# Whole-row background norms, a two-chunk join and recut last groups in a decoder trunk on one core

## The chip, the core and the metric

One core of a Trainium2 chip runs the whole program. The metric is the time of one execution in microseconds, the median of several runs. The profile is of one execution.

## The reference

A decoder trunk of one layer works on 2064 prompt rows (16 learned ones and 2048) and on 64 sample rows (8 sequences of 8), all of 1024 channels. The layer has two sub-layers with residual adds, and a final norm follows. Everything is in float32.

```python
h = rmsnorm(x, norm1_g)
z = h @ w_in                                   # 1024 -> 5120
a = za * sigmoid(zg); a = causal_dwconv(a, prev_conv, conv_dw)      # width 31
a = silu(layernorm(a + conv_b, ln_g, ln_b)) @ w_conv_out
p = multiscale_pool(zp); p = (p @ w_pool per group) * pool_scale
x = x + (sigmoid(gate_a) * a + sigmoid(gate_b) * p) @ w_out
h2 = rmsnorm(x, norm2_g)
up = causal_dwconv(h2 @ w_up, prev_ffn, ffn_dw)                     # 1024 -> 5632, width 3
x = x + (gelu(g) * v) @ w_down                                      # 2816 -> 1024
y = rmsnorm(x, final_g)                        # x * rsqrt(mean(x*x) + 1e-6) * g
```

Outputs are y for the prompt and the sample rows, and the last rows of the three histories.

## The kernel before, in words

Channels lie on the 128 partitions and rows along the free axis. The rows are cut into three blocks of 704, 704 and 708 columns (the sample rows are in the last); a block is worked through in two halves of 352 or 354 columns, which fit the two halves of one PSUM tile. Every matrix product is done as three products of high and low parts (`hi` and `lo` in the type float32r), so a weight tile holds both parts.

A *unit* is the work of one chunk of 128 output channels: 48 matmuls for a projection from 1024 channels. The list `units` is the order of TensorE's work: for each block the input projection, the convolution's output, `WO` (the output projection), `FF` (the feed-forward), with parts of the next block in between. `WO` and `FF` of the first and the last block start with half units (`SPLIT`: first half, then second half); the middle block takes both halves at once. After each unit's matmuls a *post* empties its PSUM tile (four of them) with VectorE and ScalarE operations.

`join(i)` marks all units after unit i as joined to it. Joined units are issued in turns, one step over 128 input channels of each in a turn, so that a group can begin while the norm that feeds it is still giving out its channels. Between the turns of a joined group, and after each single unit, `drip()` issues background work. In `FF` (line 1402) the first three chunks, `up(0)`, `up(FC)` and `up(1)`, are one joined group for each part.

Background work is written as generators (`Task`). They give up control with `at(ap, late)`, "not before this tile is ready, plus `late`", by the kernel's own timetable (`Pace`), and with `room(k)`, "not before k tiles of the pool `spool` are free". `CALM` is 2.5 us of `late` for norms that nobody waits for. The order of the tasks in `order` is their priority; at the end all that are left are forced in this order. Posts come first, then weight splits, then these tasks.

A norm's factor is made by `rstd_ps` (line 361): `sumsq` squares and adds the eight channel tiles; small full-precision matmuls with the sum's columns as weights give the sums for 128 rows at a time in a PSUM column; ten VectorE operations on these few columns compute the inverse root; and more small matmuls spread each value over all 128 partitions. `rstd_of` copies that to SBUF. A block of 704 or 708 columns takes six slices, a half three. Tasks with norms are `norm1_rstd` (first norm of a block), `norm2`, `final`, and `conv_norm` for the LayerNorm.

Weights come through four buffers (`W_BUFS`); SP issues their loads in order, three units ahead when the split parts are already kept in DRAM. In the last block (`MIXED`) all but the first three of the 22 feed-forward chunk pairs are made by a scheme with seven half-size products (`pair`), and the residual is kept in DRAM between the down-projections: `fetch` reads it, `spill` writes it back.

```python
MIX_GROUPS = (6, 6, 4, 3, 3)     # chunks for each down-projection of the last block
...
                    if f1 < FC - MIX_GROUPS[-1] and b in MIXED:
                        spill(b, c)
```

So in the last block a down-projection follows one pair after its chunks; the last but one and the last come after all pairs, the last one in halves (`SPLIT`). Helpers in the profile: L224 matmul, L183 tensor_tensor, L187 scalar_tensor_tensor, L192 and L194 tensor_scalar, L198 activation, L203 POOL copies, L207 loads by SP, L212 loads by POOL, L218 stores.

Of the kernel before, what the change touches and what calls it, by code (L numbers as in the profile page):

```python
# [8 lines left out]
F32 = mybir.dt.float32  # L9
F32R = mybir.dt.float32r  # L10
I32 = mybir.dt.int32
AF = mybir.ActivationFunctionType
ALU = mybir.AluOpType
# [5 lines left out]
FC = F // P  # L19
# [10 lines left out]
EPS = 1e-6  # L30
MAGIC = float(0x5F3759DF)

NBLK = 3
SBLK = 2
# [17 lines left out]
W_BUFS = 4  # L52
RAW_BUFS = 2
PLAIN = 3
MIX_GROUPS = (6, 6, 4, 3, 3)
MIX_ROOM = 4
F_GROUPS = (6, 5, 5, 6)
LEAD = 4
# [5 lines left out]
CALM = 2500.0  # L64
# [5 lines left out]
BOTH, FIRST, SECOND = (0, 1), (0,), (1,)  # L70
SPLIT = (FIRST, SECOND)
# [64 lines left out]
def trunk(ctx: ExitStack, tc: tile.TileContext, A, O):  # L136
# [15 lines left out]
    def S(cols, dt=F32, what="s"):  # L152
        assert cols <= S_COLS
        t = spool.tile([P, cols], dt, tag="s", name=nm(what))
        held.append(t)
        return t
# [3 lines left out]
    def room(k):  # L160


        def ok():
            held[:] = [t for t in held if sys.getrefcount(t) > 3]
            return len(held) + k <= S_SLOTS - RESERVE

        if not ok():
            yield "room", ok

    def PSUM():  # L170
        return pace.alloc("ps", 4, ppool.tile([P, 2, 512], F32, tag="ps", name=nm("ps")))
# [10 lines left out]
    def tt(out, a, b, op):  # L182
        nc.vector.tensor_tensor(out=out, in0=a, in1=b, op=op)  # L183
        pace.put("dve", dve(out, 68 + 60 * (b.space == "PSUM")), [out], [a, b])

    def stt(out, a, s, b, op0, op1):
        nc.vector.scalar_tensor_tensor(out=out, in0=a, scalar=s, in1=b, op0=op0, op1=op1)  # L187
        pace.put("dve", dve(out, 68 if isinstance(s, float) else 129), [out], [a, b])

    def ts(out, a, s1, s2, op0, op1=None):  # L190
        if op1 is None:
            nc.vector.tensor_scalar(out=out, in0=a, scalar1=s1, scalar2=None, op0=op0)  # L192
        else:
            nc.vector.tensor_scalar(out=out, in0=a, scalar1=s1, scalar2=s2, op0=op0, op1=op1)  # L194
        pace.put("dve", dve(out, 130, 1.92), [out], [a])

    def act(out, a, func, **kw):
        nc.scalar.activation(out, a, func, **kw)  # L198
        ptr = sum(not isinstance(v, float) for v in kw.values())
        pace.put("act", size(out) / 1.2 + 93 + 93 * ptr + 51 * (a.space == "PSUM"), [out], [a])  # L200
# [22 lines left out]
    def mm(out, lhsT, rhs, start, stop, rate=1.0, again=False):  # L223
        nc.tensor.matmul(out, lhsT=lhsT, rhs=rhs, start=start, stop=stop, skip_group_check=again)  # L224
        pace.put("pe", size(out) * rate / 2.4 + (15.5 if rate == 1.0 else 2.5), [out], [lhsT, rhs])

    cst = cpool.tile([P, NCST], F32, tag="cst", name="cst")
    half = cpool.tile([P, O_FD - O_LG], F32, tag="half", name="half")
    ones = cpool.tile([P, P], F32, tag="ones", name="ones")
    ahist = cpool.tile([P, KC, HC], F32, tag="ahist", name="ahist")  # L230
    phist = cpool.tile([P, KC, HP], F32, tag="phist", name="phist")
    hhist = [cpool.tile([P, KC, 2], F32R, tag=f"hhist{i}", name=f"hhist{i}") for i in range(2)]
# [36 lines left out]
    R = {}  # L269
# [108 lines left out]
    def at(ap, late=0.0):  # L378
        return "at", pace.ready(ap) + late
# [9 lines left out]
    def rstd_ps(src, n, late=0.0):  # L389
# [31 lines left out]
        yield at(ps)  # L421
        return ps[:, :halves, :h]

    def rstd_of(src, n, late=0.0):
        ps = yield from rstd_ps(src, n, late)
        yield from room(1)
        out = S(n)
        act(wide(out, ps), ps, AF.Copy)
        yield at(out)
        return out  # L430

    def wide(x, ps):
        return x.rearrange("p (a c) -> p a c", a=ps.shape[1])

    def sumsq(src, n):

        acc, prev = None, None
        for c in range(KC + 1):
            q = None
            if c < KC:  # L440
                s = yield from src(c)
                yield from room(1)
                q = S(n)
                act(q, s, AF.Square)
                del s
            if prev is not None:
                yield at(prev)
                if acc is None:
                    acc = prev
                else:  # L450
                    tt(acc, acc, prev, ALU.add)
            prev = q
        return acc
# [45 lines left out]
    def norm1_rstd(b):  # L499
        W = WIDTHS[b]  # L500
        yield from room(3)
        xs = [x_load(b, c) for c in range(2)]

        def src(c):
            x = xs.pop(0)
            if c + 2 < KC:
                xs.append(x_load(b, c + 2))
            yield at(x)
            return x

        R["rstd1", b] = yield from rstd_of(src, W, CALM)

    def h_make(b, last):
        while ("rstd1", b) not in R:
# [291 lines left out]
    def x_part(b, ts_, key):  # L806
        c0, c1 = cols(b, ts_)

        def src(k):
            c = order_of(ts_)[k]  # L810
            ok = lambda: all(c in R.get((key, b, t), ()) for t in ts_)
            while not ok():
                yield "cond", ok
            x = R["x1", b, c][:, c0:c1]
            yield at(x)
            return x

        return src
# [299 lines left out]
    def final(b, ts_):  # L1118
        c0, c1 = cols(b, ts_)
        last = b == NBLK - 1 and ts_[-1] == 1  # L1120
        r = yield from (rstd_ps if last else rstd_of)(x_part(b, ts_, "x2n"), c1 - c0, 0.0 if b == NBLK - 1 else CALM)
        for c in range(KC):
            x = R["x1", b, c][:, c0:c1]
            o = wide(x, r) if len(r.shape) == 3 else x
            calm = lambda: b == NBLK - 1 or pace.free["dma"] < pace.free["pe"]
            yield "room", calm
            stt(o, o, col(O_FG + c), r, ALU.mult, ALU.mult)
            store(O["y"][c, :, COL0[b] + c0 : COL0[b] + c1], x, b == NBLK - 1)
            if ts_[-1] == 1:
                del R["x1", b, c]  # L1130
            yield
# [25 lines left out]
    def join(first):  # L1157

        for u in units[first + 1 :]:
            u.joined = True  # L1160
# [197 lines left out]
    def FF(b, parts, last_parts):  # L1358

        mark["FF", b] = len(units)  # L1360
        ws = [w_up(0), w_up(FC), w_up(1)]
        holds = [[] if len(parts) > 1 else None for _ in ws]
        for ts_ in parts:
            i = len(units)
            for m, w, hold in zip((0, FC, 1), ws, holds):
                up(b, m, w, (("h2", b, ts_),), ts_, hold)
            join(i)
        nd = (("h2", b, parts[-1]),)
        f0, pend = 0, None
        for gs in MIX_GROUPS if b in MIXED else F_GROUPS:  # L1370
            for f in range(f0, f0 + gs):
                if b in MIXED and f >= PLAIN:
                    pair(b, f)
                else:
                    if f > 1:
                        up(b, f, w_up(f), nd + ((("mx", b),) if b in MIXED and f == PLAIN - 1 else ()))
                    if f:
                        up(b, FC + f, w_up(FC + f), nd)
                if f == (f0 if f0 + gs < FC or b not in MIXED else FC - 1) and pend:
                    DN(b, *pend)  # L1380
                    pend = None
            pend = (f0, f0 + gs)
            f0 += gs
        mark["up_end", b] = len(units)
        DN(b, *pend, last_parts)
# [18 lines left out]
    for b in range(NBLK):  # L1404
        if b + 1 < NBLK:
            add_task(("r1", b + 1), norm1_rstd(b + 1), mark["WO", b] if b else 2)
            add_task(("h1", b + 1), h_make(b + 1, False), mark["WO", b] if b else 0, [("r1", b + 1)])
        if b == 0:
            add_task(("cv", 0), conv_norm(0))
        add_task(("s", b), silu(b), mark["mid", b] if b else mark["C", 0] - 2, [("cv", b)])  # L1410
        for ts_ in parts.get(b, (BOTH,)):
            add_task(("h2", b, ts_), norm2(b, ts_))
        if b in MIXED:
            add_task(("mx", b), mixed_rows(b), after=[("h2", b, parts[b][-1]), ("mw",)])
        for ts_ in SPLIT if b == NBLK - 1 else (BOTH,):
            add_task(("y", b, ts_), final(b, ts_), mark["PG", b + 1] + 6 if b + 1 < NBLK else 0)
        if b + 1 < NBLK:
            add_task(("h1b", b + 1), h_make(b + 1, True), mark["up_end", b], [("r1", b + 1)])
        if b + 1 < NBLK:
            if b + 1 == SBLK:  # L1420
                for c in range(KC):
                    add_task(("sc", c), sample_conv(c))
            add_task(("cv", b + 1), conv_norm(b + 1), after=[("sc", c) for c in range(KC)] if b + 1 == SBLK else ())
# [76 lines left out]
    with tc.manual_schedule():  # L1500
# [10 lines left out]
        last = {}  # L1511
# [7 lines left out]
        i = 0  # L1519
        while i < len(units):  # L1520
# [25 lines left out]
            i = e  # L1546
# [95 lines left out]
```

## Time and profile before

| | |
|---|---|
| median of 3 runs | 2948.03 us (2946.34 to 2948.48) |
| profiled execution | 2945.39 us, span 2943.6 us, mean granted clock 0.996 |
| TensorE busy | 2902.4 us (99%), 17928 matmuls |
| VectorE busy | 2040.3 us (69%) |
| ScalarE busy | 817.5 us (28%) |
| GpSimd busy | 388.2 us (13%) |
| moved by DMA | 655.55 MB, mean 223 GB/s |

TensorE sets the time: in the chain that ended last its matmuls are 86%. To judge an edit, ask first whether it takes matmul time away, then which of TensorE's few waits it touches.

### The profile page before, as it was taken

To read this page: it belongs to the slowest core of one execution; us is meant where nothing else is said; L and a number is where in the kernel's file an instruction comes from. 1 tells how busy PE (TensorE), PEld (TensorE's weight loads), DVE (VectorE), ACT (ScalarE), POOL (GpSimd) and SP (SyncE) were. 2 spreads that over 40 slices of the span, in tenths; PEclk is the share of its full clock that TensorE was granted. 3 is DMA by queue.
4 is the path that set the end of the run, shared out by engine and by line. 5 is a ranking of instruction groups with operands and counts; after the bars stand their busy time and mean duration, and the time that the engine had idled before them with its cause. 6 is when DMAs were issued, how large, how long until landed. Compare 5 with 4: busy or idle time off the path is not lost.

```text
span 2943.6 us, 44436 instructions
## 1 busy us (share of the span) xinstructions
PE 2902.4 (99%) x17928; PEld 2895.6 (98%) x17928; DVE 2040.3 (69%) x3015; ACT 817.5 (28%) x1238; POOL 388.2 (13%) x752
## 2 busy tenths in 40 slices
PE   7999999999999999999999999999999999999998
PEld 7999999999999999999999999999999999999997
DVE  7999988679997454743498999656683136544556
ACT  4201334233223232522220212223252113221222
POOL 1111210120000001332110000223330010000000
PEclk9999999999999999999999999999999999999999
DMA  7424554865656655798644344779984365788786
GB/s 275 163 79 162 208 198 172 324 230 174 233 185 211 225 187 210 269 339 294 224 172 149 120 148 143 260 264 323 339 299 149 131 260 190 265 283 271 261 314 205
DMA packets 158397, 655.55 MB, mean 223 GB/s; under 512 B 25072, under 2 KB 37232, under 8 KB 116592
## 3 DMA queue, kind: packets, MB, share of 16 engines
q1 hardware_dynamic: 105728, 411.60, 41.7%
q0 software_dynamic: 52464, 241.11, 20.8%
q8 instruction: 141, 2.31, 0.3%
q14 instruction: 64, 0.52, 0.0%
HBM read 428.58 MB, written 224.05 MB: 222 GB/s over the span
## 4 chain that ended last, share of the span: by engine, by line
PE 86%; issue 4%; DVE 4%; DMA 3%; ACT 1%; POOL 1%; SPq 0%; DVEq 0%; POOLq 0%; ACTq 0%
PE ps L224 86%; DVE s L187 2%; POOL keep L218 1%; DMA raw<-in_w_out 1%; DVE s L183 1%; ACT s L198 1%; DVE wb L183 1%; DMA wb<-keep 1%; DMA keep<-s 1%; ACT wb L198 0%; DMA raw<-in_w_in 0%; SPq L207 0%; DMA cst<-in_cst 0%; DMA raw<-in_w_up 0%; POOL raw L212 0%
## 5 line engine op out<-in xcount | busy, mean ns | idle before, releaser
L224 PE MATMUL ps<-s,wb 128*128 128x354 f32 (+3 forms) x17628 | 2870.5, 325 | 12.6 <-DMA wb<-keep 4.1
L224 PEld LDWEIGHTS ps<-s,wb 128*128 128x128 f32 x17628 | 2858.3, 189 | 17.1 <-issue 8.7
L187 DVE SCALAR_TENSOR_TENSOR s<-s,half,s 128x704 f32<-128x704 f32 (+1 forms) x720 | 619.4, 923 | 0.3 <-ACT s L198 0.3
L198 ACT ACTIVATE s<-s 128x704 fp32r<-128x704 f32 (+10 forms) x447 | 313.5, 711 | 769.8 <-DVE s L187 484.1
L183 DVE TENSOR_TENSOR s<-s,s 128x704 fp32r<-128x704 f32 (+11 forms) x526 | 401.1, 775 | 123.4 <-ACT s L198 115.0
L183 DVE TENSOR_TENSOR s<-s,ps 128x704 f32<-128x704 f32 (+4 forms) x233 | 165.2, 720 | 251.8 <-PE ps L224 210.8
L198 ACT ACTIVATE s<-ps 128x356 f32<-128x356 f32 (+6 forms) x197 | 117.2, 601 | 658.2 <-PE ps L224 630.9
L187 DVE SCALAR_TENSOR_TENSOR s<-ps,cst,s 128x704 f32<-128x704 f32 (+1 forms) x188 | 178.1, 949 | 76.3 <-ACT s L198 72.4
L218 POOL DMA_DIRECT2D keep<-s x266 | 142.5, 541 | 587.8 <-ACT s L198 466.2
L187 DVE SCALAR_TENSOR_TENSOR s<-s,cst,s 128x708 f32<-128x708 f32 (+4 forms) x188 | 156.3, 842 | 69.2 <-ACT s L198 60.9
L183 DVE TENSOR_TENSOR wb<-raw,wb 128x1024 fp32r<-128x1024 f32 (+3 forms) x136 | 152.7, 1125 | 42.5 <-ACT wb L198 41.9
L198 ACT ACTIVATE wb<-raw 128x1024 fp32r<-128x1024 f32 (+3 forms) x136 | 132.3, 978 | 170.3 <-PE ps L224 66.4
L218 POOL DMA_DIRECT2D keep<-wb x136 | 77.1, 567 | 693.5 <-DVE wb L183 670.1
L198 ACT ACTIVATE s<-ps,cst 128x704 f32<-128x704 f32 (+1 forms) x94 | 78.9, 842 | 262.8 <-PE ps L224 257.4
L183 DVE TENSOR_TENSOR s<-raw,s 128x512 fp32r<-128x512 f32 x114 | 75.1, 686 | 95.6 <-ACT s L198 63.6
L187 DVE SCALAR_TENSOR_TENSOR s<-s,ps 128x704 f32<-128x704 f32 (+6 forms) x66 | 43.9, 685 | 132.8 <-PE ps L224 121.4
L187 DVE SCALAR_TENSOR_TENSOR s<-s,s 128x704 f32<-128x704 f32 (+2 forms) x96 | 84.8, 886 | 44.3 <-ACT s L198 42.6
L198 ACT ACTIVATE s<-raw 128x512 fp32r<-128x512 f32 x114 | 68.6, 625 | 124.9 <-DMA raw<-in_w_up 92.7
L183 DVE TENSOR_TENSOR s<-s 128x718 f32<-128x718 f32 (+6 forms) x64 | 55.0, 859 | 29.8 <-ACT s L198 22.5
L218 POOL DMA_DIRECT2D out_ffn_s<-sf x44 | 23.7, 538 | 301.6 <-ACT sf L198 250.2
L187 DVE SCALAR_TENSOR_TENSOR sc<-sa,cst,sc 128x64 f32<-128x64 f32 x232 | 46.9, 276 | 1.0 <-ACT sc L198 0.7
L198 ACT ACTIVATE s<-s,half 128x704 f32<-128x704 f32 (+1 forms) x48 | 46.4, 972 | 0.8
(62 smaller groups left out, 470.8 us busy)
## 6 DMA issues: line engine op xcount, KB each, us to landing
wb<-keep SPq DMA_DIRECT2D x225, 1024.0 KB, 4.9
keep<-wb POOLq DMA_DIRECT2D x100, 1024.0 KB, 6.5
keep<-s POOLq DMA_DIRECT2D x266, 256.0 KB, 5.1
wb<-keep SPq DMA_DIRECT2D x32, 768.0 KB, 4.8
raw<-in_w_up SPq DMA_DIRECT2D x44, 512.0 KB, 4.1
raw<-in_w_in SPq DMA_DIRECT2D x40, 512.0 KB, 4.6
raw<-in_w_up POOLq DMA_DIRECT2D x38, 512.0 KB, 9.2
wb<-keep SPq DMA_DIRECT2D x35, 512.0 KB, 4.7
```

Source lines behind the costliest of these rows:

```text
L183: nc.vector.tensor_tensor(out=out, in0=a, in1=b, op=op)
L187: nc.vector.scalar_tensor_tensor(out=out, in0=a, scalar=s, in1=b, op0=op0, op1=op1)
L198: nc.scalar.activation(out, a, func, **kw)
L218: (nc.sync if last else nc.gpsimd).dma_start(out=dst, in_=src)
L224: nc.tensor.matmul(out, lhsT=lhsT, rhs=rhs, start=start, stop=stop, skip_group_check=again)
```

## The change

It has five edits. `rstd_wide` makes a norm's factor on whole rows: `mean_of` splits the sum of squares into a high and a low part and multiplies each by a matrix of 1/1024, so that the mean stands on all partitions at once, with two products for each half; the inverse root is then computed on all columns by VectorE, with two squares on ScalarE. Three norms use it: the first norm of the last block, and the final norms of the first two blocks. The final norms of the last block keep the old helpers. `join(i)` is called after the second chunk of `FF`, so that `up(1)` follows as a unit of its own in each part. The down-projections of the last block take 6, 6, 3, 3 and 4 chunks. And the tasks for the two halves of the last block's final norm are listed second half first.

```diff
-MIX_GROUPS = (6, 6, 4, 3, 3)
+MIX_GROUPS = (6, 6, 3, 3, 4)
...
+    ones_r = ones.bitcast(F32R)
...
+    def mean_of(x, n):
+
+        yield from room(2)
+        hi, lo = S(n, F32R), S(n, F32R)
+        act(hi, x, AF.Copy)
+        yield at(hi)
+        tt(lo, x, hi.bitcast(F32), ALU.subtract)
+        yield at(lo, CALM)
+        ps = PSUM()
+        k = 1 if n <= 512 else 2
+        for t in range(k):
+            c = slice(t * (n // k), (t + 1) * (n // k))
+            mm(ps[:, t, : n // k], ones_r, lo[:, c], True, False)
+            mm(ps[:, t, : n // k], ones_r, hi[:, c], False, True)
+        return ps[:, :k, : n // k]
+
+    def rstd_wide(src, n):
+
+        acc = yield from sumsq(src, n)
+        yield at(acc)
+        ps = yield from mean_of(acc, n)
+        del acc
+        yield at(ps)
+        yield from room(4)
+        v, m, r = S(n), S(n), S(n)
+        ts(wide(v, ps), ps, EPS, None, ALU.add)
+        ts(r.bitcast(I32), v.bitcast(I32), -0.5, MAGIC, ALU.mult, ALU.add)
+        act(m, r, AF.Square)
+        yield at(m)
+        stt(m, m, -1.0, v, ALU.mult, ALU.mult)
+        q = S(n)
+        ts(q, m, 0.375, 1.25, ALU.mult, ALU.add)
+        yield
+        tt(q, q, m, ALU.mult)
+        stt(r, q, 1.875, r, ALU.add, ALU.mult)
+        act(m, r, AF.Square)
+        yield at(m)
+        stt(m, m, -0.5, v, ALU.mult, ALU.mult)
+        stt(r, m, 1.5, r, ALU.add, ALU.mult)
+        yield at(r)
+        return r
...
-        R["rstd1", b] = yield from rstd_of(src, W, CALM)
+        R["rstd1", b] = yield from (rstd_wide(src, W) if b == SBLK else rstd_of(src, W, CALM))
...
     def final(b, ts_):
-        r = yield from (rstd_ps if last else rstd_of)(x_part(b, ts_, "x2n"), c1 - c0, 0.0 if b == NBLK - 1 else CALM)
+        if b == NBLK - 1:
+            r = yield from (rstd_ps if last else rstd_of)(x_part(b, ts_, "x2n"), c1 - c0)
+        else:
+            r = yield from rstd_wide(x_part(b, ts_, "x2n"), c1 - c0)
...
             for m, w, hold in zip((0, FC, 1), ws, holds):
                 up(b, m, w, (("h2", b, ts_),), ts_, hold)
-            join(i)
+                if m == FC:
+                    join(i)
...
-        for ts_ in SPLIT if b == NBLK - 1 else (BOTH,):
+        for ts_ in SPLIT[::-1] if b == NBLK - 1 else (BOTH,):
             add_task(("y", b, ts_), final(b, ts_), mark["PG", b + 1] + 6 if b + 1 < NBLK else 0)
```

## The prediction

> **What bounds the kernel now.** I read the page, then TensorE's table of waits, then the timeline around each wait, the windows of granted clock and the last chain.
>
> ```profile
> span 2943.6 us, 44436 instructions
> PE 2902.4 (99%) x17928; PEld 2895.6 (98%) x17928; DVE 2040.3 (69%) x3015; ACT 817.5 (28%) x1238; POOL 388.2 (13%) x752
> DVE  7999988679997454743498999656683136544556
> PE ps L224 <- DVE s L183: 14.4, 3, 10.1
> PE ps L224 <- DVE rs L187: 7.5, 6, 2.0
> PE ps L224 <- DMA wb<-keep: 4.1, 3, 2.5
> PE ps L224 <- issue: 3.9, 1, 3.9
> ```
>
> TensorE is busy 2902.4 of 2943.6 us. So only three things are worth time: matmul time taken out, one of its few waits removed, or the ends. VectorE is at 69% as a mean, but its digits stand at 8 and 9 in the 20th to 24th slices (1470 to 1840 us): there it can be the limit itself.
>
> **The change part by part.** The profiled execution took 2945.39 us (span 2943.6), 2.64 us under the median of the runs, 2948.03. The sum is made against 2945.39, and 2.64 is added at the end.
>
> *a. The three norms.* The old helper puts two bundles of small matmuls into TensorE's stream, the new one a single bundle of four products.
>
> ```profile
> 1425.19 1.39 PE L224 MATMUL ps<-ones,s 128*128 128x1 f32 x12
> 1426.44 7.93 PE L224 MATMUL ps<-s,wb 128*128 128x352 f32 x48
> 1434.21 1.50 PE L224 MATMUL ps<-cst,rs 128*128 128x128 f32 x12
> 1435.47 1.85 PE L224 MATMUL ps<-s,wb 128*128 128x352 f32 x10
> 2448.96 0.16 DVE L192 TENSOR_SCALAR rs<-ps 128x3 f32<-128x3 f32 x1 [6.85 <-PE ps L224]
> ```
>
> This is the norm of the last block's input, in TensorE's timeline (start, length, form, count). From the first small matmul to the next large one: 1426.44-1425.19 = 1.25 us, and 1435.47-1434.21 = 1.26 us, so 2.51 us. The other two norms cut as many columns into the same six slices, so they cost the same. The new products are like those of the second row: 7.77 us (1426.44 to 1434.21) for 48, so 0.162 us each and 0.65 us for four. Upper bound: 0.30 us each, as the full-precision row-sum products below (four records in 1.36 us, the last pipelined), so 1.2 us. I take 0.65, because operands and shape are those of the 0.162 row. Saving 3 x (2.51-0.65) = **-5.6**, by the upper bound -3.9.
>
> VectorE and ScalarE pay for it. VectorE's ten operations on six columns (0.16 us each, 0.2 apart) become nine on 704 or 708 columns, at most 0.95 us each (first DVE row of part c): at most 8.5 us in place of 2, three times. That is hidden by VectorE's idle time in the 17th, 20th and 30th slices (digits 7, 4, 8). If the cover were gone, up to 6.5 us each would be exposed. The new helper issues no DMA. It asks for two, then four free tiles of the pool, where the old one asked for one.
>
> *b. First block's feed-forward, two chunks joined.* While the joined group runs, the norm of the second half puts in its sums, and one turn of the group later its broadcast. A turn is nine matmuls with three chunks, six with two.
>
> ```profile
> 2448.78 1.72 PE L224 MATMUL ps<-s,wb 128*128 128x356 f32 x9
> 2450.96 0.93 PE L224 MATMUL ps<-cst,rs 128*128 128x128 f32 x6 [0.46 <-DVE rs L187]
> 620.99 0.93 PE L224 MATMUL ps<-cst,rs 128*128 128x128 f32 x6 [0.48 <-DVE rs L187]
> ```
>
> In the last block and in the first, nine matmuls did not quite cover VectorE's chain of ten small operations. Three matmuls less are 0.49 us more of that wait: **+0.5**. In the middle block the norm lies under other work.
>
> *c. Middle block's feed-forward.*
>
> ```profile
> 1603.75 15.29 DVE L187 SCALAR_TENSOR_TENSOR s<-s,half,s 128x644 f32<-128x644 f32 x19
> 1618.95 3.78 DVE L187 SCALAR_TENSOR_TENSOR s<-ps,cst,s 128x704 f32<-128x704 f32 x4
> 1620.99 9.25 PE L224 MATMUL ps<-s,wb 128*128 128x354 f32 x46 [3.86 <-issue]
> 1620.99:1625.67 4.68, 4.68 (x20) 4.68 (x21) 2.94 (x4) 1.94 (x3) 0.00 (x0) 0.64 0.06 26
> 2444.63:2447.80 3.17, 3.17 (x11) 3.17 (x12) 0.00 (x0) 0.00 (x0) 0.00 (x0) 0.54 0.96 397
> ```
>
> The "issue" wait of 3.86 us is VectorE's: TensorE's fifth chunk needs the PSUM buffer of the first (four buffers), and VectorE reads that one only at 1618.95 (two operations, to 1620.85), after 19 taps of the convolution. Three joined chunks end together and leave one chunk (7.8 us) until the fifth; two end a chunk earlier and leave two, and the first chunk's operations are issued a chunk earlier too. So this wait goes. After it the granted clock was 0.64 for 4.68 us, with 20 matmuls where 28.7 would fit at 0.163 us: 1.4 us more. Gone: 5.3 us.
>
> What is late next is VectorE itself, which has no idle time up to the convolution's LayerNorm:
>
> ```profile
> 1817.42 3.42 DVE L183 TENSOR_TENSOR s<-s,s 128x704 f32<-128x704 f32 x4
> 1824.57 1.36 PE L224 MATMUL ps<-s,ones 128*128 128x354 f32 x4
> 1844.54 3.52 DVE L183 TENSOR_TENSOR s<-s,s 128x708 f32<-128x708 f32 x4
> 1850.00 1.40 PE L224 MATMUL ps<-ones,s 128*128 128x1 f32 x12
> ```
>
> The sum for the mean is ready by 1820.84 and used at 1824.57: 3.7 us of room. That for the variance is ready at 1848.06 and used at 1850.0 (its weight loads some 0.15 earlier): 1.8 us. A TensorE 5.3 us earlier waits 1.6 us at the first and 1.9 at the second, so 3.5 us come back: -1.8. Up to 1.4 us more return if the clock falls after such a wait. I take the middle, **-1.2**; ends -5.3 (room enough) and 0. The Trainium skill, "TensorE: Matmul & The Clock Gate", section "What's actually happening", says that the clock halves after an idle window of about 3.4 us. By it waits of under 2 us would cost only themselves, so -1.8 and a sum 0.6 lower; the trace shows 0.54 after a spell whose longest wait was 2.5 us, which the page alone does not give, so I keep the middle.
>
> *d. Last block's feed-forward.*
>
> ```profile
> 2432.61 4.23 SPq L207 DMA_DIRECT2D wb<-keep  x2
> 2441.36 0.72 PE L224 MATMUL ps<-s,wb 128*128 128x356 f32 x3 [0.49 <-DMA wb<-keep]
> 2444.63 3.67 PE L224 MATMUL ps<-s,wb 128*128 128x356 f32 x12 [2.54 <-DMA wb<-keep]
> ```
>
> The joined group wants three weight tiles at once, and four buffers hold them and the chunk before. The third is issued by SP only when a buffer comes free, at about 2436.5, and TensorE waits 2.54 us for it. With two joined it is needed 24 x 2 matmuls (7.8 us) after the group's start: the 2.54 go. So does the clock of 0.54 (11 matmuls in 3.17 us, 19.4 would fit: 1.4 us). The second tile's 0.49 stays. As in b, the broadcast waits 0.5 longer. **-3.4** (2.54+1.4-0.5); ends -4.4 (the broadcast's 0.46 goes as well) and -2.0 (the clock falls all the same).
>
> *e. Last groups 6 6 3 3 4.* As many matmuls. But the third down-projection now has three chunks with a fetch and a spill of the residual beside it; before, the three-chunk groups had no spill.
>
> ```profile
> wb<-keep SPq DMA_DIRECT2D x35, 512.0 KB, 4.7
> wb<-keep SPq DMA_DIRECT2D x23, 384.0 KB, 4.0
> s<-xd SPq DMA_DIRECT2D x32, 354.0 KB, 6.0
> xd<-s POOLq DMA_DIRECT2D x32, 354.0 KB, 6.7
> 2778.86:2810.11 31.25, 31.25 (x193) 31.25 (x193) 13.68 (x20) 3.15 (x8) 4.86 (x9) 1.00 0.93 335
> GB/s 275 163 79 162 208 198 172 324 230 174 233 185 211 225 187 210 269 339 294 224 172 149 120 148 143 260 264 323 339 299 149 131 260 190 265 283 271 261 314 205
> ```
>
> The window is the old third group: 1220 KB (1.25 MB) per unit of 24 matmuls (3.9 us), 320 GB/s, and 335 measured at a share of 0.93. New: 1092 KB (1.12 MB) per 18 matmuls (2.93 us), 382 GB/s. Eight units at 335 GB/s take 26.7 us against 23.4 on TensorE: 3.3 us if every byte had to arrive in time, 0 if the lag is only the spills', for which nobody waits. I take **+1.0**, nearer to 0, because weights are loaded three units ahead. The Trainium skill, "DMA: Bandwidth & Descriptors", section "Where 436 GB/s comes from", gives about 358 GB/s from HBM per core; by that the stage would need 25.0 us, an estimate of +1.6 for this term. The trace's highest slice, 339, does not contradict it.
>
> *f. The tail.*
>
> ```profile
> 2919.68 0.93 PE L224 MATMUL ps<-cst,rs 128*128 128x128 f32 x6 [0.46 <-DVE rs L187]
> 2928.20 0.54 DVE s L183
> 2929.26 0.54 DVE s L183
> 2929.89 0.54 DVE s L183
> 2930.53 0.54 DVE s L183
> 2931.16 0.54 DVE s L183
> 2931.84 0.81 PE ps L224 x6
> ```
>
> After the last large matmul the chain holds VectorE's residual add (2928.20), a square, and four adds of squares, 0.63 apart: three are backlog, left because VectorE took the first half's output before them. With the second half's task ahead of the first's, and 1.95 us in place of 1.47 per unit to do both, one add remains: -1.9. The wait of 0.46 at the broadcast of the first half goes too, since a unit is now 12 matmuls. **-2.4**; end 0.
>
> Sum: -5.6+0.5-1.2-3.4+1.0-2.4 = -11.1. So 2934.3 against 2945.39, and with the 2.64, **2936.9 us**.
>
> **The rivals.**
>
> 1. *VectorE has room at the LayerNorm.* For it: the norm's place among the chunks is set by the kernel's own timetable, and one chunk later is 7.8 us of room. Against: the timetable hardly differs. Then c is -5.3 and, with e at 0, the sum -16.2: 2931.8.
>
> 2. *Most of the waits only move.* For it: 3.5 of 5.3 us already come back in c; e could cost 3.3; if the reordered tail still leaves the adds behind, f is 0. With c at 0, f at 0 and e at 3.3: -5.6+0.5-3.4+3.3 = -5.2, 2942.8. If the products cost 0.30 us as well, 2944.5.
>
> 3. *Slower, through the tile pool.* The wide norms hold up to five more of 52 tiles, in the stage after a feed-forward where tiles are short. If a tile is then taken before its reader is done, VectorE waits for a TensorE instruction to come. Bounds for such a wait: nothing, and the longest wait on VectorE in TensorE's table, 10.1 us. It decides if two of them, at the end, fall on the LayerNorm chain of the last block or on the convolution's output: 20.2-11.1 = 9.1 slower, 2957. One does not turn the sign. Against: TensorE's table has three such waits in all, of 14.4 us together.
>
> **How the numbers follow.** About 0.2%, 5.9 us, is what a measurement can tell. Forecast (c to f near their values) 0.55, rival 1 0.2, rival 2 0.19, rival 3 0.06. The forecast and rival 1 are faster; of rival 2, some 0.03 is over the bound. So 0.78 faster, 0.16 same, 0.06 slower. The range runs from all terms at their good ends (-5.6+0.5-5.3-4.4+0-2.4 = -17.2: 2930.8), less 1.5 for the scatter of runs, to rival 2's upper value.
>
> **What would show it.** a: at the three places four `ps<-s,ones` products with 0.65 us to the next large matmul, and no `rs` operations. b: the wait before the broadcast in the first block near 1 us. c: no 3.9 us "issue" wait, and a new wait of TensorE on VectorE before the last block's LayerNorm sums. d: no wait for `wb<-keep` of 2.5 us and no dip of the granted clock at the last feed-forward. e: the window of the 15th chunk's down-projection over 350 GB/s, with a wait for `wb<-keep` of a few us or none. f: one add between the last square and the column sums, 1.9 us less from the last large matmul to the end. The prediction is wrong if VectorE's backlog grows ahead of the middle feed-forward, or if tiles run short.

## The result, and the profile after

The changed kernel takes 2931.05 us (median of 4 runs, 2929.41 to 2932.28) against 2947.19 us (4 runs, 2944.79 to 2948.48) for the kernel before on the same chip: ratio 0.994, interval [0.9926, 0.9953], 16.1 us faster. The prediction was 2936.9 us, 11.1 us faster. The result lies in its range, near its lower end, and close to the time of the first rival (2931.8).

The first lines are from the page of the changed kernel, the next TensorE's table of waits (total, count, longest).

```profile
span 2927.6 us, 44319 instructions
...
PE 2893.1 (99%) x17868; PEld 2886.8 (99%) x17868; DVE 2056.1 (70%) x3012; ACT 822.7 (28%) x1244; POOL 392.4 (13%) x752
```

```profile
PE ps L224 <- DVE s L183: 13.7, 5, 9.5
PE ps L224 <- DVE rs L187: 8.0, 5, 2.0
PE ps L224 <- ACT s L198: 3.6, 2, 1.9
PE ps L224 <- DMA wb<-keep: 1.6, 4, 1.0
```

The span fell by 16.0 us, TensorE's busy time by 9.3. There are 60 matmuls fewer: in each of the three norms 24 small ones became four. The "issue" wait of 3.9 us is gone, and so is the 2.5 us wait for `wb<-keep`. VectorE has 15.8 us more to do.

To see where the time went, count TensorE's large matmuls (`ps<-s,wb`) in both traces, which run in the same order, and take the difference of the start times of the same one. What that difference gains or loses over a stretch is called a *step* here; its last tenth depends on where the stretch is taken to begin and end. The steps of the changed kernel, with the prediction's letters:

| stretch | forecast | step |
|---|---|---|
| a: three wide norms | -5.6 | -2.11, -1.77, -2.12: -6.0 |
| b: first feed-forward, joined group | +0.5 | +0.48, and -0.95 spread over the chunks behind it |
| c: middle feed-forward, and the LayerNorm after it | -1.2 | -3.98, -1.61, then +1.85: -3.7 |
| d: last feed-forward | -3.4 | -4.16 |
| e: third down-projection | +1.0 | +2.20 |
| f: from the first of the last two groups to the end | -2.4 | -2.4 |
| everything else (all of it ahead of the first feed-forward) | 0 | -1.4 |

The -1.4 is scatter: the same kernel, run again in experiment 9, is 0.7 us behind the kernel before at that place.

The next rows are TensorE's timeline of the changed kernel at the places that the prediction showed (start, length, form, count, wait before it): the first feed-forward's broadcast (b), a norm (a), the middle feed-forward and the LayerNorm's sums (c), the last feed-forward (d), the third down-projection (e) and the end (f). Behind them stand two windows, at c and e (length, busy time and count of TensorE, its weight loads, VectorE, ScalarE and GpSimd, granted clock, DMA share, GB/s).

```profile
619.05 0.94 PE L224 MATMUL ps<-cst,rs 128*128 128x128 f32 x6 [0.95 <-DVE rs L187]
...
1177.69 0.81 PE L224 MATMUL ps<-s,ones 128*128 128x352 f32 x4
1178.34 3.88 PE L224 MATMUL ps<-s,wb 128*128 128x352 f32 x23
...
1603.70 18.56 PE L224 MATMUL ps<-s,wb 128*128 128x354 f32 x113
...
1841.06 1.47 PE L224 MATMUL ps<-ones,s 128*128 128x1 f32 x12 [1.69 <-DVE s L183]
...
2429.76 2.68 PE L224 MATMUL ps<-s,wb 128*128 128x356 f32 x15 [0.17 <-DVE s L183]
...
2435.04 0.94 PE L224 MATMUL ps<-cst,rs 128*128 128x128 f32 x6 [0.97 <-DVE rs L187]
...
2774.19 4.12 PE L224 MATMUL ps<-s,wb 128*128 128x356 f32 x24 [1.03 <-DMA wb<-keep]
...
2915.41 1.11 PE L224 MATMUL ps<-ones,s 128*128 128x1 f32 x6 [1.80 <-DVE s L183]
2918.56 1.65 PE L224 MATMUL ps<-cst,rs 128*128 128x128 f32 x6 [2.04 <-DVE rs L187]
```

```profile
1843.00:1850.00 7.00, 7.00 (x45) 7.00 (x44) 2.19 (x9) 0.00 (x0) 0.00 (x0) 1.00 0.39 126
2771.00:2801.00 30.00, 28.63 (x174) 27.85 (x173) 12.68 (x22) 7.04 (x16) 2.15 (x4) 1.00 0.96 376
```

Four products and 0.65 us (1178.34-1177.69) stand where two bundles cost 2.51. From 1603.70 to 1622.26 TensorE runs through, where it had waited 3.86 us. The wait before the variance's column sums (1841.06) is new, but the clock stays at 1.00 after it. At the last feed-forward only the broadcast waits, but for 0.17 us at the start. The third down-projection waits for a weight tile although 376 GB/s flow.

One thing the prediction did not look at also changed. These rows are VectorE's timeline in the convolution of the last block's input: first the kernel before, then the changed one.

```profile
1484.70 1.01 DVE L187 SCALAR_TENSOR_TENSOR s<-s,ps 128x354 f32<-128x354 f32 x3
...
1579.17 1.02 DVE L187 SCALAR_TENSOR_TENSOR s<-s,ps 128x354 f32<-128x354 f32 x3 [7.09 <-PE ps L224]
```

```profile
1481.45 1.02 DVE L187 SCALAR_TENSOR_TENSOR s<-s,ps 128x354 f32<-128x354 f32 x3 [1.50 <-ACT s L198]
...
1568.49 1.01 DVE L187 SCALAR_TENSOR_TENSOR s<-s,ps 128x354 f32<-128x354 f32 x3
...
1600.21 3.77 DVE L187 SCALAR_TENSOR_TENSOR s<-ps,cst,s 128x704 f32<-128x704 f32 x4
```

These are the posts that empty a convolution input's PSUM tile. Before, one of them waited 7.09 us for a matmul issued after those that filled its PSUM tile. That matmul gives it no data, so what the post needs from it can only be the room it writes to, a tile of the pool that the matmul still reads. After, the same post does not wait, and VectorE comes to the first PSUM tile of the middle feed-forward at 1600.21, not at 1618.95. So there are two candidates for what ended the 3.86 us wait: the shorter join, and a VectorE that is no longer late.

### The profile page after: what moved, and what is told of

The parts are those of the page before. It is cut to its first block, busy times and chain, and to the rows that moved or that the text cites. A ratio compares the mean times of both kernels' runs of the same rounds, so it can differ in the third digit from the quotient of the medians.

```text
span 2927.6 us, 44319 instructions
## 1 busy us (share of the span) xinstructions
PE 2893.1 (99%) x17868; PEld 2886.8 (99%) x17868; DVE 2056.1 (70%) x3012; ACT 822.7 (28%) x1244; POOL 392.4 (13%) x752
## 4 chain that ended last, share of the span: by engine, by line
PE 77%; issue 12%; DVE 5%; DMA 3%; POOL 1%; ACT 0%; SPq 0%; DVEq 0%; POOLq 0%; ACTq 0%
PE ps L224 77%; DVE s L187 3%; DMA raw<-in_w_up 2%; DVE sc L187 1%; POOL keep L218 1%; DMA wb<-keep 1%; DVE s L183 1%; ACT s L198 0%; DMA keep<-s 0%; SPq L207 0%; DMA s<-in_x 0%; DMA s<-xd 0%; DVE rs L187 0%; POOL raw L212 0%; DVE raw L183 0%
## 5 line engine op out<-in xcount | busy, mean ns | idle before, releaser
L198 ACT ACTIVATE s<-s 128x704 f32<-128x704 f32 (+10 forms) x456 | 320.2, 713 | 762.4 <-DVE s L187 464.4
L183 DVE TENSOR_TENSOR s<-s,s 128x704 f32<-128x704 f32 (+11 forms) x532 | 406.4, 778 | 121.3 <-ACT s L198 113.0
L187 DVE SCALAR_TENSOR_TENSOR s<-s,s 128x704 f32<-128x704 f32 (+2 forms) x108 | 95.8, 887 | 32.2 <-ACT s L198 30.1
```

## The experiments

In experiments 1 to 4 the kernel before had 2947.03 us (17 runs), in 5 to 8 2948.53 (9 runs), in 9 to 12 2947.9 (9 runs). Where only one run was made its steps are read, not its time: single runs scatter by several us, in these traces mostly near 2080 and 2160 us and at the last feed-forward. Where a bracket lists kernels, a number is that of an experiment, and *after* is the first profile of the changed kernel.

**1. The norms alone.** `rstd_wide`, `mean_of` and their two callers as in the change; join, groups and order as before.

> Only the three wide norms; join, groups and task order as before. Theory A (the join removed the wait at the middle feed-forward): 3 x 1.86 = 5.6 us less matmul time, the 3.9 us wait of TensorE at the middle feed-forward stays with its 1.6 us of slow clock; time about 2941.5. Theory B (the wait came from a 7.1 us wait of VectorE for a pool tile during the last block's convolution input, and the norm's extra tiles shift which tile is taken): the 7.1 us wait of VectorE is gone, and so is TensorE's 3.9 us wait without any join; up to 1.9 us come back at the LayerNorm sums; time about 2938.

Measured: 2939.65 us (10 runs), ratio 0.997 [0.996, 0.998]. The 7.1 us wait of VectorE is gone, and with it, under the old join, TensorE's "issue" wait (steps -3.97 and -1.59). At the LayerNorm 1.62 us came back:

```profile
1603.81 21.36 PE L224 MATMUL ps<-s,wb 128*128 128x354 f32 x130
...
1842.25 1.47 PE L224 MATMUL ps<-ones,s 128*128 128x1 f32 x12 [1.61 <-DVE s L183]
```

So the norms suffice to end the wait in c. But about 100 us later this kernel lost 2.5 us again, at a wait for which the profile shows no cause:

```profile
1949.77 5.55 PE L224 MATMUL ps<-s,wb 128*128 128x352 f32 x33 [2.24 <-issue]
```

Only the two kernels with the wide first norm and the old join lose time there (1 and 6); the cause is open.

**2. The join alone.** (In the kernel before, `FF` stands at line 1358 and `rstd_ps` at line 389, not at the lines given with the description.)

```diff
-            join(i)
+                if m == FC:
+                    join(i)
```

> Only the join of two chunks. Both theories: +0.5 us at the first feed-forward (broadcast waits 0.97 instead of 0.48), -3.9 at the last one (no 2.5 us wait for weights, no dip of the clock). At the middle one theory A: VectorE still waits 7.1 us for a tile, TensorE's 3.9 us wait is gone all the same, and 3.5 us come back as waits at the LayerNorm sums, net about -2; time about 2942.5. Theory B: with the 7.1 us wait left, VectorE is so late that TensorE still waits at the fifth chunk, 2 us or more; time about 2944.

Measured: 2938.11 us (8 runs), ratio 0.9968 [0.9957, 0.9979], over 4 us less than either theory had it. VectorE's wait stays, at 7.22 us, and the "issue" wait goes all the same (-4.02, -1.65). The first row is VectorE's timeline, the others TensorE's, and the last a window behind the LayerNorm's sums:

```profile
1578.43 1.02 DVE L187 SCALAR_TENSOR_TENSOR s<-s,ps 128x354 f32<-128x354 f32 x3 [7.22 <-PE ps L224]
```

```profile
1603.83 21.37 PE L224 MATMUL ps<-s,wb 128*128 128x354 f32 x131
...
1844.61 1.93 PE L224 MATMUL ps<-ones,s 128*128 128x1 f32 x12 [1.06 <-DVE s L183]
```

```profile
1846.40:1852.20 5.80, 5.80 (x21) 5.80 (x22) 1.67 (x10) 0.00 (x0) 0.00 (x0) 0.50 0.37 147
```

So the join suffices to end that wait too: the two edits take the same 5.6 us. Here 4.2 us came back: the wait was shorter than in the changed kernel, but the granted clock was 0.50 for 5.8 us after it. The step at the last feed-forward was -3.74.

**3. The groups alone.**

```diff
-MIX_GROUPS = (6, 6, 4, 3, 3)
+MIX_GROUPS = (6, 6, 3, 3, 4)
```

> Only the groups 6 6 3 3 4. The third down-projection costs 2.2 us of waits for weights as in the changed kernel (theory A: too dense traffic of three-chunk units with fetch and spill; rival: nothing here, the waits came from the other edits shifting loads). In the tail, if the longer units alone give VectorE time for its backlog, the time from the last large matmul to the end falls by 1.4 us or more as with all edits; if the task order does it, the tail stays at 15.8 us.

One run, span 2948.8 us. The third down-projection loses 2.32 us, with this wait on TensorE's timeline, and from the last large matmul to the end it takes 13.9 us in place of 15.8:

```profile
2795.60 6.68 PE L224 MATMUL ps<-s,wb 128*128 128x356 f32 x38 [1.53 <-DMA wb<-keep]
```

So the groups alone cause the loss in e, and the longer units of the last group alone clear VectorE's backlog of adds.

**4. The order of the last two tasks alone.**

```diff
-        for ts_ in SPLIT if b == NBLK - 1 else (BOTH,):
+        for ts_ in SPLIT[::-1] if b == NBLK - 1 else (BOTH,):
```

> Only the second half's final norm listed first. If the order clears the backlog: one add after the last square in place of four, from the last large matmul to the end about 1.9 us less. If the units of three chunks are too short for VectorE's work (15.4 us of work in 11.7 us), the first half's outputs move into the tail instead and the end comes within 0.7 us of before.

One run, span 2945.3 us. The end is 1.39 us shorter: TensorE's wait before the last column sums fell from 3.68 us (first row, the kernel before) to 2.27 (second row):

```profile
2931.84 0.80 PE L224 MATMUL ps<-ones,s 128*128 128x1 f32 x6 [3.68 <-DVE s L183]
...
2933.54 0.80 PE L224 MATMUL ps<-ones,s 128*128 128x1 f32 x6 [2.27 <-DVE s L183]
```

So groups (-1.86) and order (-1.40) each take nearly the whole -1.43 of the changed kernel after the last large matmul. The rest of f, 1.0, lies ahead of it.

**5. Does a shift in the rotation of the tile pool end VectorE's wait?** The kernel before, with six small tiles taken and dropped after the first norm of the last block.

```diff
+        if b == SBLK:
+            for _ in range(6):
+                pcopy(S(1), ones[:, :1])
```

> The kernel before, with six one-column tiles taken from the pool and written by POOL after the first norm of the last block, and nothing else. Theory B (which tile the convolution's input takes follows from how many were taken before): VectorE's 7.1 us wait during the last block's convolution input is gone or has another length, and with it the 3.9 us wait of TensorE at the middle feed-forward; up to 3.5 us come back at the LayerNorm sums. Rival (the wait went because the wide norm changed VectorE's timing there): the 7.1 us wait and the 3.9 us wait both stand as before.

One run, span 2956.0 us, the longest of all; 7.3 us of the loss came near 2160 us and 5.1 at the last feed-forward. VectorE's wait stays, and TensorE's too (3.84), so a shift by six tiles does not end it:

```profile
1579.64 1.02 DVE L187 SCALAR_TENSOR_TENSOR s<-s,ps 128x354 f32<-128x354 f32 x3 [7.23 <-PE ps L224]
```

**6. Only the last block's first norm wide; 7. only the two final norms wide.**

```diff
# 6
-        R["rstd1", b] = yield from rstd_of(src, W, CALM)
+        R["rstd1", b] = yield from (rstd_wide(src, W) if b == SBLK else rstd_of(src, W, CALM))
# 7
+        if b == NBLK - 1:
+            r = yield from (rstd_ps if last else rstd_of)(x_part(b, ts_, "x2n"), c1 - c0)
+        else:
+            r = yield from rstd_wide(x_part(b, ts_, "x2n"), c1 - c0)
```

> Of the three wide norms only that of the last block's input. 1.86 us of matmul time less there, none at the two final norms. Theory B: the 7.1 us wait of VectorE is gone, since this norm takes six more tiles just ahead of the last block's tiles. Rival (the final norms did it): the wait stands, 7.1 us.

> Of the three wide norms only the final ones of the first two blocks: 2 x 1.86 us of matmul time less. If the shift of tiles by the last block's norm alone matters, the 7.1 us wait of VectorE and TensorE's 3.9 us wait stand as before; if any shift of tiles earlier moves it too, they are gone here as well.

One run each, spans 2943.9 and 2943.3 us. In 6 VectorE's wait and TensorE's are gone (-3.99, -1.62; +1.85 came back), and the norm gave -2.04; but 5.3 us were lost between 1945 and 1960 us, where experiment 1 lost 2.5, so that the span is that of before. In 7 the norms gave -2.02 and -2.03, and both waits stay:

```profile
1576.34 1.02 DVE L187 SCALAR_TENSOR_TENSOR s<-s,ps 128x354 f32<-128x354 f32 x3 [7.09 <-PE ps L224]
```

```profile
1618.18 7.13 PE L224 MATMUL ps<-s,wb 128*128 128x354 f32 x33 [3.82 <-issue]
```

So it is the first norm of the last block that ends VectorE's wait.

**8. A group of four with the fetch, and a group of two.** The changed kernel with

```diff
-MIX_GROUPS = (6, 6, 3, 3, 4)
+MIX_GROUPS = (6, 6, 4, 2, 4)
```

> The changed kernel with groups 6 6 4 2 4: the third down-projection, which fetches and spills, is back at four chunks for a unit (320 GB/s asked in place of 382), and the fourth, without a spill, has two. The 2.2 us of waits for weights at the third down-projection go; at the fourth 256 and 354 KB come for each 1.95 us (320 GB/s), so little or no wait. About 2 us less than the changed kernel's 2931.05, 2929; if the two-chunk units starve instead, the same as the changed kernel or 1 to 2 us more.

Measured: 2936.28 us (5 runs), ratio 0.9958 [0.9944, 0.9972], some 5 us over the changed kernel. The third down-projection lost nothing (step -0.24 in place of +2.20), but the fourth lost 6.16. TensorE's timeline there, a window, and VectorE's timeline just ahead:

```profile
2876.73 7.51 PE L224 MATMUL ps<-s,wb 128*128 128x354 f32 x31 [3.93 <-DVE s L183]
```

```profile
2876.00:2881.00 5.00, 4.27 (x14) 4.27 (x15) 3.40 (x5) 0.00 (x0) 0.00 (x0) 0.50 0.15 57
```

```profile
2874.98 0.90 DVE L183 TENSOR_TENSOR s<-s,s 128x708 fp32r<-128x708 f32 x1 [0.86 <-ACT s L198]
2875.79 2.49 DVE L183 TENSOR_TENSOR s<-s,ps 128x708 f32<-128x708 f32 x3
```

A unit of two chunks is 12 matmuls, about 2 us, and VectorE was still at the posts of the last pair when these units began: the chain that ended last holds, from 2859.8 to 2876.7, only VectorE and ScalarE in turn. The residual adds came after them (2875.79), and TensorE stood until the first was done.

**9 to 11. The changed kernel again; with the old groups; with the old groups and the old order.** In 10 `MIX_GROUPS` is 6, 6, 4, 3, 3 again, in 11 the order of the two tasks is as before too, so that norms and join are left.

> The changed kernel once more, as the measure for the next two in the same place. Theory A (the result stands): 2931 us, 2929 to 2934, and the same steps: third down-projection 2.2 us later (2.0 to 2.5), 1.9 us back at the variance sum, tail 14.3 us from the last large matmul. Theory B (part of the -16 us was a run without scatter): 2935 us or more, with a wait or a slow spell that the first profile did not have.

> The changed kernel with the groups of the kernel before (6 6 4 3 3); the order of the last two tasks stays as changed. Theory A (terms add): the 2.2 us at the third down-projection are gone, and the tail keeps most of its gain because the order alone gave 1.39 us of 1.43: 1 to 2.5 us under the changed kernel, about 2929. Theory B (the shorter last groups are needed with the other edits in place): the tail loses 1 us or more, and the time is that of the changed kernel or up to 2 us over it.

> Norms and join alone: groups and order of the kernel before. Theory A: the third down-projection as before, the tail as before (15.8 us from the last large matmul to the end, 1.4 more than changed), so about 0.8 us under the changed kernel by 2.2-1.4: 2930; 1.4 us over the kernel with the order alone changed. Theory B (groups and order matter together): over the changed kernel by 1 us or more.

Measured, 5 runs each: 2931.86 us (ratio 0.9944 [0.993, 0.9958]), 2932.12 (0.9947 [0.9932, 0.9962]) and 2932.44 (0.9945 [0.9929, 0.9962]). They can't be told apart. Norms and join bring the whole gain that can be measured. Groups and order take something at the end and give it back at the third down-projection: without the new groups its step is -0.24 (10 and 11), with them +1.44 in 9. From there to the end 9 gains 2.1 us, 10 0.9, and 11 loses 0.8. That the 10th would win 1 to 2.5 us over the changed kernel and the 11th 0.8, as theory A had it, did not come true, nor did the loss of 1 us or more that theory B had for the 11th.

All three lost more at the LayerNorm than the first profile of the changed kernel: 3.5, 5.1 and 3.4 us, after waits of 1.79, 1.78 and 1.70. The windows behind it, of 9, 10 and 11:

```profile
1844.50:1851.50 7.00, 7.00 (x35) 7.00 (x36) 2.13 (x12) 0.00 (x0) 0.00 (x0) 0.76 0.28 108
```

```profile
1844.50:1851.50 7.00, 7.00 (x31) 7.00 (x32) 1.67 (x10) 0.00 (x0) 0.00 (x0) 0.64 0.15 55
```

```profile
1844.50:1851.50 7.00, 7.00 (x36) 7.00 (x35) 1.97 (x8) 0.00 (x0) 0.00 (x0) 0.76 0.20 60
```

**12. The wide norm's hold on the pool without its arithmetic.** The kernel before; the last block's first norm takes four tiles and gives them back.

```diff
+        if hold:
+            yield from room(4)
+            extra = [S(n) for _ in range(4)]
+            for e in extra:
+                pcopy(e[:, :1], ones[:, :1])
         if late:
             yield at(r, late)
+        for e in extra:
+            pcopy(e[:, :1], ones[:, :1])
+        del extra
```

> The kernel before; in the first norm of the last block four more tiles of 704 columns are asked for after the small operations, touched by GpSimd (one column, twice) and given back before the broadcast: the wide norm's hold on the pool without its arithmetic. Theory A (the hold on the pool moves the tiles): VectorE's 7.1 us wait near 1579 us goes, with it TensorE's 3.9 us wait at the middle feed-forward, and about 1.6 to 1.9 us come back at the LayerNorm: 3.5 to 4 us faster. Theory B (it is the time at which the norm ends, or its task's steps, that move them): both waits stay, 7.1 and 3.9 us, and the time is that of before.

One run, span 2947.1 us. Both waits stay:

```profile
1578.30 1.02 DVE L187 SCALAR_TENSOR_TENSOR s<-s,ps 128x354 f32<-128x354 f32 x3 [7.02 <-PE ps L224]
```

```profile
1620.11 6.17 PE L224 MATMUL ps<-s,wb 128*128 128x354 f32 x22 [3.78 <-issue]
```

So a hold of four tiles alone is not it either. What goes with the wait is the order of VectorE's work: in every kernel with the wide first norm (after, 1, 6 and 8 to 11) the first post of the convolution is issued ahead of the last splits of the middle block's `norm2` (1481.45 above), in all others (before, 2 to 5, 7 and 12) behind them (1484.70). That this order settles which tile the later post is given is argued, not shown.

## Why the prediction was right, and where it was off

In the profile the sum of the steps is 4.9 us beyond the forecast: c gave 2.5 more than its -1.2, the scatter ahead of the first feed-forward 1.4, the gain behind b 0.95, d 0.8 and a 0.4, and e took 1.2 back. So about half of it lies in the prediction's own terms.

- **a, the norms: right.** 0.64 to 0.65 us for four products, so 0.162 each, as taken from the large matmuls' row; three steps of -1.8 to -2.1 against -1.9 each. VectorE's longer chain, 0.53 to 0.89 us an operation, cost nothing there. (The prediction's bound of 0.95 us is a quarter of 3.78, the second VectorE row of its part c, not the first.)
- **b: right in its place.** +0.48 against +0.5. That the chunks behind it would gain 0.95 in all joined kernels (after, 2 and 8 to 11) was not foreseen; it comes in small parts all along from 630 to 1170 us, and its cause is open.
- **c: right in sign, its return mis-sized, its cause only half seen.** The wait and the slow clock went (-5.6 against -5.3). The prediction had VectorE without any idle time and so let 3.5 us of it come back, at both sums. In the profiled run only 1.85 came back, at the variance alone; the changed kernel's second profile has 3.5, and 10 and 11 5.1 and 3.4, the slow clock included. So the term is -3.7 in one execution and -0.5 to -2.2 in the others. That -1.2 lies among them is partly luck, for it was worked out from two waits, of which one did not come. The step that failed is the reading of why VectorE was late: a 7.09 us wait for a tile had made it late, not its load alone. The rivals named a tile wait that the wide norms would cause; the wide norm took one away.
- **d: right in mechanism, too small, and this is where the median moved beyond the sum.** In the profile the step is -4.16 against -3.4, because the first `wb<-keep` wait (0.49) went too. But the profiled execution of the kernel before was a mild one here. All seven other kernels with the old join (1, 3, 4, 5, 6, 7 and 12) lost more at this place than it did, by 0.6 to 5.1 us, 1.35 in the middle; all six with the new join (after, 2 and 8 to 11) lie between -3.7 and -4.4. In 3 and 4 the program is that of before up to this place, and they lost 1.35 and 2.43. So the join is worth about 5 us here. The prediction had added the 2.64 us between the profiled execution and the median to both sides as a constant. That part of those 2.64 us was this very wait, which the change takes away, is argued from the other kernels; no execution of the kernel before at its median was profiled.
- **e: too small.** +2.20 and +1.44 against +1.0. The mechanism is the one named: TensorE waits for `wb<-keep`, as experiment 3 shows for the groups alone. The 335 GB/s was not the most that could flow: 376 and 366 GB/s flowed in the changed kernel over 30 us, under the 382 that TensorE could have used. The prediction compared its bounds with the slices of the page, at most 339, and passed over the 397 GB/s of its own window at 2444.63, in part c.
- **f: right in sum (-2.4).** One add is left after the last square: VectorE's operation at 2914.74 runs just behind ScalarE's square, which ends at 2914.71. But half of the cause was superfluous, since either edit clears most of the backlog. Against the kernel without them, groups and order together bring 0.6 us by the medians (9 against 11), less than can be measured.

The Trainium skill, "TensorE: Matmul & The Clock Gate", section "What's actually happening", has the clock halve after an idle window of about 3.4 us. By it none of the waits at the LayerNorm should have cost more than itself. The windows at 0.50 to 0.76 after waits of 1.06 to 1.79 us differ from that, and the measurement decides.

What stays open: which part of the wide norm moves the tile wait (neither a shift by six tiles nor a hold on four does), and how much norms and join share. Alone they bring 7.4 and 8.9 us, 16.3 in all, and together 15.5. By the traces c is -4.0 in experiment 1, -1.4 in 2 and -2.2 in 11, so with c counted once the two would bring some 13. The 2.5 us that 1 loses near 1950 us, and the kernels with both edits do not, would make up most of the rest; one trace does not show that, and the intervals of the three ratios (about 3 us either way for the first two, 5 for the third) don't exclude 13 either.

## What to carry to other kernels

Before a wait is put down to an engine's load, follow that engine back to its own last idle time: a single wait for a buffer 40 us earlier can be the cause, and then two unrelated edits each remove the same loss and their gains don't add. The difference between a profiled execution and the median is itself made of waits: look in the traces of sibling kernels where they scatter, and if the change removes that wait, it can remove the scatter with it. Edits that only exchange one end of a stage for another, as groups and order did here, should be timed against the kernel without them before they are kept.

## What was not expected of the hardware

The granted clock fell after short waits, and not every time. After a wait of 1.06 us it was 0.50 for 5.8 us (experiment 2), after 1.78 us 0.64 over 7 us (10), and after 1.79 and 1.70 us 0.76 (9 and 11). After 1.69 us in the first run of the changed kernel, which is the kernel of 9, it stayed at 1.00, as after 1.61 (1) and 1.91 (6), the longest of them. So much the same instructions after much the same wait cost nothing more (within 0.2 us) or 1.7 to 3.3 us, and the length of the wait does not decide it.
